# Attention scores of two heads in the two halves of TensorE's rows, and attention in rounds

## The chip, the cores and the metric

The kernel runs on one core of one Trainium2 chip. The metric is the device time of one execution in microseconds; the time of a kernel is the median of its runs. Engine names are those of the profile: PE is TensorE's matmul, PEld its weight load, DVE VectorE, ACT ScalarE, POOL GpSimd, SP the queue engine that issues most DMAs.

## What is computed

One layer of a hybrid decoder on x (1, 512, 1024), in float32:

```python
h = rms_norm(x, norm_w);  proj = h @ w_in                     # 1024 -> 4096, eight parts of 512
hq, hf, hi, hg, aq, ak, av, ag = split(proj)
o_h = rms_norm(hgrn2(hq, hf, hi)) * silu(hg)                  # 4 heads, gated linear recurrence
q, k = rms_norm(heads(aq)), rms_norm(heads(ak))               # 8 heads of width 64
s = q @ k.T * 64**-0.5 - slope * (t - s_pos);  causal         # 512 keys: own block of 256 and all past ones
o_a = softmax(s) @ heads(av) * silu(ag)
out = x + concat(o_h, o_a) @ w_out
```

With 512 positions and blocks of 256 a query's own block and its selected past blocks are all keys up to its position, so the attention is plain causal attention with a distance penalty (ALiBi).

## The kernel before

Tokens are cut in four tiles of 128, and everything large goes through TensorE. To keep float32 precision at the speed of the format fp32r, an operand is split into a high part (rounded to fp32r by ScalarE) and a low part (the rest, by VectorE), and a product is a sum of passes: high x high, high x low, low x high. Projections are eight groups of four units (`group`, `unit`); a unit accumulates 8 x 3 passes of 512 columns in one PSUM bank. The last groups are K (group 5), Q (6) and V (7); after them comes the output product in two parts, `out_h` for the recurrence's half of the mixed width and `out_a` for attention's half.

**The order on TensorE is written out** by a small planner inside the kernel: each pass adds its planned time to `clock[0]`, the projections and `out_h` are a filler that yields after every three passes (planned 0.648), and side work runs in generators (threads) that name the time and the `done` keys they wait for. Before each filler step, `drive` runs a thread that is ready by the planner's clock; when the filler is at its end, it advances the clock to the next thread. A `done` key holds the planner's time at which the instructions were issued. The other engines' queues are ordered by a scheduler at build time. At run time each engine works through its queue in order and waits at semaphores.

**K and Q.** `ev_qk` normalizes a unit's 128 tokens, and 14.29 later on the planner's clock `qk_tr` transposes them (four transpositions into one PSUM tile). Rows 0 to 63 of the result belong to the even head of each pair, rows 64 to 127 to the odd one. For each of the two heads of a pair (j) ScalarE and VectorE write high and low parts on 64 partitions, and a DMA on SP's queue copies them to the other 64: so the K tile of a head holds K high twice, KL holds K low twice, and the Q tile holds Q high over Q low. One pass over 128 rows then gives (Qhigh + Qlow) Khigh, and another (Qhigh + Qlow) Klow.

**Attention** goes by pairs of heads (p = 0 to 3) and units c = 3p + (0, 1, 2): query tile 3 (512 keys), tile 2 (384), tiles 1 and 0 (256 + 128). Each unit is one thread (`attn_unit`): scores of the two heads (`mm` into PSUM tiles `sc`, pool `psc` of four banks); minimum with the bias on VectorE (line 665), exponential with its sum on ScalarE (668), reciprocal on VectorE (671), product on GpSimd (673); then transpositions into two `tp` tiles of the pool `ptr` (two banks, line 55), copied by ScalarE to SBUF (682); then products with V, each head writing its half of the columns of `ot` (697). The units are spawned when the filler has gone through V (`start_attention`, line 951), a unit's scores wait by the planner for the transpositions of two units before, and products come for two units together. When all four tiles of a pair are done, VectorE multiplies `ot` by the gate (706) and the result is split for the output product (707, 708).

Lines that the change touches or that the prediction speaks of: 55, 148 (`LAT`), 568 to 589 (`qk_tr`), 597 to 621, 623 to 629, 635 to 715, 733 to 747 (`out_fin`: the residual's loads on GpSimd's and SP's queues, into the buffer that `hTl` leaves after V), 872, 949 to 953.

Of the kernel before, what the change touches and what calls it, by code (L numbers as in the profile page):

```python
# [1 line left out]

# [6 lines left out]
F32 = mybir.dt.float32  # L9
F32R = mybir.dt.float32r  # L10
I32 = mybir.dt.int32
AF = mybir.ActivationFunctionType
ALU = mybir.AluOpType
# [8 lines left out]
def kernel(  # L22
# [35 lines left out]
    def scratch(dt=F32):  # L58
        return scr.tile([P, 512], dt, tag="scr", name="scr")
# [85 lines left out]
            split_lo(n)  # L145

    POOL_LO = (3,)
    LAT = dict(lm=4.544, lev0=9.2567, lev=4.4882, copy=1.9908, rms=5.7036, silu=15.1764, qk=14.2881, soft=2.5598, softn=0.0041, acopy=4.5215, st=1.5748, ch=6.6909, DEPTH=2)
    SEQ = ('v0 y7 nt A0 s00 k00 y1 s10 k10 a0 H00 H10 B0 b0 H01 H11 t10 l10 L00 L10 L01 L11 wh1 t01 p20 q20 wl1 l01 '
           't11 p30 q30 l11 p01 q01 t02 p11 q11 l02 wh2 t12 l12 p21 q21 wl2 t03 l03 p31 q31 sq0 wh3 p02 q02 wl3 sq1 '  # L150
           't13 l13 p12 q12 sq2 p22 q22 sq3 rs p32 q32')
# [416 lines left out]
    def qk_tr(key, u, nrm, gain):  # L568
        yield LAT["qk"]
        tp = ptr.tile([P, 512], F32, tag="tr", name="tp")  # L570
        for j in range(NP):
            tr(tp[:, j * P:(j + 1) * P], nrm[:, j * P:(j + 1) * P])
        tpr = tp.rearrange("p (j t) -> p j t", t=P)
        ts_ = slice(u * P, (u + 1) * P)
        low = None if key == "K" else scratch(F32R).rearrange("p (j t) -> p j t", t=P)
        for j in range(2):
            lo = A["KL", j][:, :, ts_] if key == "K" else low
            own = slice(j * DH, (j + 1) * DH)
            oth = slice((1 - j) * DH, (2 - j) * DH)
            dst = A[key, j]  # L580
            nc.scalar.activation(dst[own, :, ts_], tpr[own], AF.Copy, scale=gain[own])
            nc.vector.scalar_tensor_tensor(lo[own], tpr[own], gain[own], dst[own, :, ts_].bitcast(F32),
                                           op0=ALU.mult, op1=ALU.subtract)
            if key == "K":
                for z in (dst, A["KL", j]):
                    nc.sync.dma_start(out=z[oth, :, ts_].bitcast(F32), in_=z[own, :, ts_].bitcast(F32))
            else:
                nc.sync.dma_start(out=dst[oth, :, ts_].bitcast(F32), in_=lo[own].bitcast(F32))
        done[(key, u)] = clock[0]

    A = {}
# [5 lines left out]
    def ev_qk(key, tags, gain):  # L597
        def ev(u, ps):
            if u == 0:
                wait_for("chunks")  # L600
                if key == "K":
                    for j in range(2):
                        A[key, j] = big.tile([P, NP, T], F32R, tag=tags[j], name=f"{key}{j}")
                        A["KL", j] = big.tile([P, NP, T], F32R, tag=tags[2 + j], name=f"KL{j}")
                else:
                    Q = big.tile([P, 2, NP, T], F32R, tag=tags[0], name=key)
                    for j in range(2):
                        A[key, j] = Q[:, j]
            sq = scratch()
            nc.scalar.activation(sq, ps, AF.Square, scale=rst[:, u:u + 1])  # L610
            ss = small.tile([P, 8], F32, tag="ss8", name="ss8")
            nc.vector.tensor_reduce(ss, sq.rearrange("p (h e) -> p h e", e=DH), axis=AX.X, op=ALU.add)
            r = rstd_of(ss, DH, 8)
            r2 = small.tile([P, 8], F32, tag="r2", name="r2")
            nc.gpsimd.tensor_tensor(r2, r, rst[:, u:u + 1].to_broadcast([P, 8]), op=ALU.mult)
            nrm = scratch()
            nc.vector.tensor_tensor(nrm.rearrange("p (h e) -> p h e", e=DH),
                                    ps.rearrange("p (h e) -> p h e", e=DH),
                                    r2.unsqueeze(2).to_broadcast([P, AH, DH]), op=ALU.mult)
            spawn(qk_tr(key, u, nrm, gain))  # L620
        return ev

    def ev_v(u, ps):
        if u == 0:
            wait_for(*[("read", n) for n in range(NT)])
            A["v"] = big.tile([P, NT, 512], F32, tag="G", name="vt")
        nc.scalar.activation(A["v"][:, u, :], ps, AF.Copy, scale=rst[:, u:u + 1])
        if u == 1:
            nc.scalar.activation(warm, A["v"][:, u, 0:1], AF.Exp, scale=0.0)


    UNITS = ((3,), (2,), (1, 0))
    DEPTH = LAT.get("DEPTH", 2)

    def attn_unit(c, p, tiles, ctx_):
        need = [("K", u) for u in range(tiles[0] + 1)] + [("Q", i) for i in tiles]
        if c >= DEPTH:
            need.append(("sdone", c - DEPTH))
        yield (0.0, *need)
        if "bias" not in ctx_:  # L640
            bias = big.tile([P, 2, T], F32, tag="at", bufs=2, name="bias")
            for j in range(2):
                nc.gpsimd.tensor_scalar(bias[:, j, :], A["Dm"], 2.0 ** (-8.0 * (2 * p + j + 1) / AH), 1.0,
                                        op0=ALU.mult, op1=ALU.mult)
            ctx_["bias"] = bias
        bias = ctx_["bias"]
        cols = []
        at = 0
        for i in tiles:
            cols.append((i, at, (i + 1) * P))  # L650
            at += (i + 1) * P
        m = len(tiles)
        zs = []
        for j in range(2):
            sc = psc.tile([P, 512], F32, tag="sc", name="sc")
            for i, o, n in cols:
                ts_ = slice(i * P, (i + 1) * P)
                us = max(0.109, n / 2370.0)
                mm(sc[:, o:o + n], A["Q", j][:, p, ts_], A["K", j][:, p, 0:n], True, False, us)
                mm(sc[:, o:o + n], A["Q", j][:, p, ts_], A["KL", j][:, p, 0:n], False, True, us)  # L660
            z = scratch()
            nm = small.tile([P, 2], F32, tag="nm", name="nm")
            l = small.tile([P, 2], F32, tag="l", name="l")
# [7 lines left out]
            nc.vector.reciprocal(rl[:, 0:m], l[:, 0:m])  # L671
            for e, (i, o, n) in enumerate(cols):
                nc.gpsimd.tensor_scalar(z[:, o:o + n], z[:, o:o + n], rl[:, e:e + 1], 1.0, op0=ALU.mult, op1=ALU.mult)  # L673
            zs.append(z)
        yield LAT["soft"] + at * LAT["softn"]
        pts = []
        for j in range(2):
            tp = ptr.tile([P, 512], F32, tag="tr", name="tp")
            for s in range(at // P):
                tr(tp[:, s * P:(s + 1) * P], zs[j][:, s * P:(s + 1) * P])  # L680
            pt = scratch()
            nc.scalar.copy(pt[:, 0:at], tp[:, 0:at])
            pts.append(pt)
        done[("sdone", c)] = clock[0]

        yield (LAT["acopy"], ("sdone", c | 1), *[(7, u) for u in range(tiles[0] + 1)])
        if "ot" not in ctx_:
            ctx_["ot"] = psc.tile([P, 512], F32, tag="sc", name="ot")
            ctx_["left"] = NT
        ot = ctx_["ot"]  # L690
        vt = A["v"]
        for i, o, n in cols:
            ts_ = slice(i * P, (i + 1) * P)
            for s in range(i + 1):
                for j in range(2):
                    hc = slice((2 * p + j) * DH, (2 * p + j + 1) * DH)
                    mm(ot[j * DH:(j + 1) * DH, ts_], vt[:, s, hc], pts[j][:, o + s * P:o + (s + 1) * P],
                       s == 0, s == i, 0.115)
        ctx_["left"] -= m
        if ctx_["left"] == 0:  # L700
            if "a" not in mT:
                mTa = big.tile([P, 2, NP, T], F32R, tag="hTh", name="mTa")
                mT["a"] = (mTa[:, 0], mTa[:, 1])
            mTah, mTal = mT["a"]
            mx = scratch()
            nc.vector.tensor_tensor(mx, ot, gT[:, p, :], op=ALU.mult)
            nc.scalar.copy(mTah[:, p, :], mx)
            nc.vector.tensor_sub(mTal[:, p, :], mx, mTah[:, p, :].bitcast(F32))
            done[("pair", p)] = clock[0]

    def start_attention():
        for p in range(NP):
            c_ = {}
            for m, tiles in enumerate(UNITS):
                spawn(attn_unit(p * len(UNITS) + m, p, tiles, c_))


    res = {}
# [146 lines left out]
    def fill_a():  # L865
        const_tri()
        yield from group(1, True, ev_f)
        yield from group(2, True, ev_silu_t(q2[:, 0]))
        yield from group(3, False, ev_silu(G))
        yield from group(4, True, ev_silu_t(gT))  # L870
        const_dist()
        yield from group(5, False, ev_qk("K", ("f", "k", "i", "KL"), kgs))
        yield from group(6, False, ev_qk("Q", ("q",), qgs))
        yield from group(7, False, ev_v)

    with tc.manual_schedule(engines={mybir.EngineType.PE}):
# [71 lines left out]

        def filler():
            yield from fa  # L950
            start_attention()
            wait_for(*[("read", n) for n in range(NT)])
            yield from out_h()

# [30 lines left out]
```

## Time and profile before

| | |
|---|---|
| runs | 290.51 us median of 3 (290.44 to 290.64) |
| profiled execution | 290.15 us, its span 288.3 us |
| granted TensorE clock | 1.00 |
| TensorE busy | 283.4 us, 98% of the span |
| VectorE, ScalarE, GpSimd busy | 173.3, 131.9, 63.4 us |
| passes and other matmul records | 1947 |

Matmul records overlap (a pass of 512 columns is listed with 0.39 us and follows the one before by 0.23), so a busy share of TensorE tells that it always had work, and the time a pass costs is read from the distance of starts or from the chain of waits, whose pieces do not overlap. Other records overlap a little as well.

### The profile page before, as it was taken

Reading aid. Unit: us, or ns where it says so; the run is one execution under the profiler, and the core shown is the slowest. Engines: PE = TensorE matmul, PEld = TensorE weight load, DVE = VectorE, ACT = ScalarE, POOL = GpSimd, SP = SyncE. Lnnn points to the kernel's source line nnn. Section 1 sums busy time; section 2 is a strip of 40 time slices with the busy share of each in tenths; the row PEclk is TensorE's granted clock in tenths of the full one; section 3 lists DMA queues with packets and bytes.
Section 4 is the critical chain, followed back from the end, with each engine's and each line's share of the span. In section 5 each row is a group of like instructions: output and inputs, shape, how many; then the busy total and the mean of one; then the engine's idle time right before and its main releaser. Section 6 shows DMA issues by size and latency. Waiting matters only on the chain.

```text
span 288.3 us, 5069 instructions
## 1 busy us (share of the span) xinstructions
PE 283.4 (98%) x1947; PEld 235.0 (82%) x1947; DVE 173.3 (60%) x374; ACT 131.9 (46%) x244; POOL 63.4 (22%) x102
## 2 busy tenths in 40 slices
PE   8999999999999999999999999999999999999995
PEld 6788788888887777898888888888888888888884
DVE  2952743734899998167855785485384677543232
ACT  5469623611601484125521743654675797652000
POOL 5006001191000000010273223420034655320000
PEclk9999999999999999999999999999999999999999
DMA  7990682430440008000610099558279000000132
GB/s 239 322 378 9 25 229 77 166 126 0 154 142 2 2 13 279 5 0 9 226 59 0 15 250 198 122 144 230 48 194 328 8 2 0 2 2 2 73 112 106
DMA packets 22152, 31.00 MB, mean 108 GB/s; under 512 B 1764, under 2 KB 9712, under 8 KB 22128
## 3 DMA queue, kind: packets, MB, share of 16 engines
q1 hardware_dynamic: 21056, 28.58, 34.7%
q0 software_dynamic: 512, 1.05, 1.2%
q10 hardware_dynamic: 560, 1.05, 1.0%
q8 instruction: 15, 0.25, 0.3%
q14 instruction: 9, 0.07, 0.1%
HBM read 25.17 MB, written 2.10 MB: 95 GB/s over the span
## 4 chain that ended last, share of the span: by engine, by line
PE 96%; DVE 1%; DMA 1%; issue 0%; ACT 0%; SPq 0%
PE acc L200 76%; PE tp L204 7%; PE sc L200 3%; PE ot L200 3%; PE pl L200 3%; PE ops L200 2%; DMA vec<-in_norm_w_dram 1%; PE us L200 1%; DVE wlo L124 0%; ACT hTh L304 0%; DVE hTl L293 0%; DVE res L781 0%; SPq L75 0%; DVE hTl L312 0%; DVE part L826 0%
## 5 line engine op out<-in xcount | busy, mean ns | idle before, releaser
L200 PE MATMUL acc<-whi,hTh 128*128 128x512 f32 x160 | 65.2, 407 | 0.0
L200 PE MATMUL acc<-whi,hTl 128*128 128x512 f32 x160 | 62.9, 393 | 0.3 <-DVE hTl L293 0.2
L200 PE MATMUL acc<-wlo,hTh 128*128 128x512 f32 x160 | 59.8, 391 | 0.0
L138 DVE TENSOR_TENSOR wlo<-raw,whi 128x1024 fp32r<-128x1024 f32 x38 | 46.1, 1236 | 7.1 <-ACT whi L130 6.6
L130 ACT CAST whi<-raw 128x1024 fp32r<-128x1024 f32 x39 | 40.5, 1048 | 13.6 <-DMA raw<-in_w_in_dram 6.2
L190 POOL TENSOR_TENSOR r<-v,mh 128x8 f32<-128x8 f32 (+1 forms) x12 | 17.2, 1430 | 99.2 <-DVE v L188 99.1
L200 PE MATMUL acc<-hTh,whi 128*128 128x512 f32 x96 | 38.2, 397 | 0.0
L200 PE MATMUL acc<-hTh,wlo 128*128 128x512 f32 x96 | 37.5, 391 | 0.0
L200 PE MATMUL acc<-hTl,whi 128*128 128x512 f32 x96 | 37.4, 389 | 0.0
L200 PEld LDWEIGHTS acc<-whi,hTl 128*128 128x128 f32 x160 | 30.1, 188 | 7.6 <-DVE hTl L312 0.9
L200 PEld LDWEIGHTS acc<-whi,hTh 128*128 128x128 f32 x160 | 30.1, 188 | 6.0
L200 PEld LDWEIGHTS acc<-wlo,hTh 128*128 128x128 f32 x160 | 30.0, 188 | 5.7
L673 POOL TENSOR_SCALAR scr<-scr,rl 128x512 f32<-128x512 f32 (+3 forms) x32 | 17.7, 562 | 18.4 <-DVE rl L671 14.8
L200 PEld LDWEIGHTS acc<-hTh,wlo 128*128 128x128 f32 x96 | 18.0, 188 | 4.0 <-DVE wlo L138 0.2
L200 PEld LDWEIGHTS acc<-hTh,whi 128*128 128x128 f32 x96 | 18.0, 188 | 3.6
L200 PEld LDWEIGHTS acc<-hTl,whi 128*128 128x128 f32 x96 | 18.0, 188 | 3.5
L745 DVE TENSOR_TENSOR res<-acc,res 128x512 f32<-128x512 f32 x15 | 10.3, 690 | 17.3 <-PE acc L200 14.6
L200 PE MATMUL acc<-whi,mTa 128*128 128x512 f32 (+1 forms) x72 | 20.4, 367 | 0.0
L668 ACT ACTIVATE scr<-scr,nm 128x512 f32<-128x512 f32 (+3 forms) x32 | 17.7, 555 | 3.4 <-DVE nm L665 2.0
L204 PE MATMUL tp<-ident,scr 128*128 128x128 f32 x128 | 18.2, 275 | 0.0
L204 PEld LDWEIGHTS tp<-ident,scr 128*128 128x128 f32 x128 | 14.9, 140 | 3.1 <-issue 0.7
L665 DVE CUSTOM_DVE_ANT_0 scr<-sc,bias 128x512 f32<-128x512 f32 (+3 forms) x32 | 14.1, 485 | 4.9 <-PE sc L200 4.9
(148 smaller groups left out, 430.8 us busy)
## 6 DMA issues: line engine op xcount, KB each, us to landing
raw<-in_w_in_dram SPq DMA_DIRECT2D x30, 512.0 KB, 4.7
raw<-in_w_out_dram SPq DMA_DIRECT2D x8, 512.0 KB, 6.0
out_dram<-res SPq DMA_DIRECT2D x7, 256.0 KB, 2.1
x<-in_x_dram SPq DMA_DIRECT2D x8, 128.0 KB, 4.3
x<-in_x_dram SPq DMA_DIRECT2D x4, 256.0 KB, 5.0
K<-K SPq DMA_DIRECT2D x8, 128.0 KB, 6.4
KL<-KL SPq DMA_DIRECT2D x8, 128.0 KB, 5.9
Q<-scr SPq DMA_DIRECT2D x8, 128.0 KB, 2.4
```

Source lines behind the costliest of these rows:

```text
L130: nc.scalar.copy(hi, raw)
L138: eng.tensor_sub(lo, raw, hi.bitcast(F32))
L190: nc.gpsimd.tensor_tensor(r, v, mh[:, 0:n], op=ALU.pow)
L200: nc.tensor.matmul(o, a, b, start=start, stop=stop)
L204: nc.tensor.transpose(o, a, ident)
L665: nc.vector.tensor_tensor_reduce(out=z[:, o:o + n], in0=sc[:, o:o + n], in1=bias[:, j, T - n:T], op0=ALU.add, op1=ALU.min, scale=1.0, scal ...
L668: nc.scalar.activation(z[:, o:o + n], z[:, o:o + n], AF.Exp, bias=nm[:, e:e + 1], scale=-1.0, accum_out=l[:, e:e + 1])
L673: nc.gpsimd.tensor_scalar(z[:, o:o + n], z[:, o:o + n], rl[:, e:e + 1], 1.0, op0=ALU.mult, op1=ALU.mult)
L745: nc.vector.tensor_tensor(res[hf][:, u, :], ps, res[hf][:, u, :], op=ALU.add)
```

## The change

- **Layout of K and Q.** `qk_tr` writes high and low parts for all 128 partitions at once: one ScalarE and one VectorE instruction for each tile of K or Q in place of two and two. The DMAs between partitions go. K, KL (buffers `f`, `k`) and Q, QL (halves of `q`) hold the two heads of a pair in the two halves of the partitions.
- **Scores.** A head's tile is three passes over its own 64 rows (Q K, Q KL, QL K), the two heads of a pair alternating, each in its own PSUM tile.
- **Rounds.** One thread, `attention`, spawned at the second unit of V (in `ev_v`), works in eight rounds of two units: products with V for the units of two rounds before, scores of this round's units, gate of the products, transpositions and copies of the round before's units, softmax of this round's. Round 0 waits by the planner for all units of K and Q with no added time, round 1 comes 5.0 after it, later ones 4.0 after the one before and after V's last unit.
- **ScalarE's order.** The exponentials of a round are bound behind its last copy of transposed tiles (`issue_after`).
- **Products** go to tiles of the pool `ptr` and are gated and split for each unit, in place in the gate's tile; the copies of transposed tiles go to buffers `i` and `KL`.

```diff
-        for j in range(2):
-            lo = A["KL", j][:, :, ts_] if key == "K" else low
...
-            nc.scalar.activation(dst[own, :, ts_], tpr[own], AF.Copy, scale=gain[own])
-            nc.vector.scalar_tensor_tensor(lo[own], tpr[own], gain[own], dst[own, :, ts_].bitcast(F32),
-                                           op0=ALU.mult, op1=ALU.subtract)
-            if key == "K":
-                for z in (dst, A["KL", j]):
-                    nc.sync.dma_start(out=z[oth, :, ts_].bitcast(F32), in_=z[own, :, ts_].bitcast(F32))
-            else:
-                nc.sync.dma_start(out=dst[oth, :, ts_].bitcast(F32), in_=lo[own].bitcast(F32))
+        hi, lo = A[key], A[key + "L"]
+        nc.scalar.activation(hi[:, :, ts_], tpr, AF.Copy, scale=gain)
+        nc.vector.scalar_tensor_tensor(lo[:, :, ts_], tpr, gain, hi[:, :, ts_].bitcast(F32),
+                                       op0=ALU.mult, op1=ALU.subtract)
...
         if u == 1:
             nc.scalar.activation(warm, A["v"][:, u, 0:1], AF.Exp, scale=0.0)
+            spawn(attention())
...
+    def scores(c):
...
+        scs = [psc.tile([P, 512], F32, tag="sc", name="sc") for _ in range(2)]
+        for i, o, n in cols:
+            ts_ = slice(i * P, (i + 1) * P)
+            for t, (a, b) in enumerate((("Q", "K"), ("Q", "KL"), ("QL", "K"))):
+                for j in range(2):
+                    own = slice(j * DH, (j + 1) * DH)
+                    mm(scs[j][:, o:o + n], A[a][own, p, ts_], A[b][own, p, 0:n], t == 0, t == 2,
+                       max(0.055, n / 4740.0))
...
+    def turn(c):
...
+            pts[m] = big.tile([P, 4, 512], F32, tag=("i", "KL")[m % 2], name="pt")
         for j in range(2):
             tp = ptr.tile([P, 512], F32, tag="tr", name="tp")
+            z = zs.pop((c, j))
             for s in range(at // P):
+                tr(tp[:, s * P:(s + 1) * P], z[:, s * P:(s + 1) * P])
+            last = nc.scalar.copy(pts[m][:, 2 * (c % 2) + j, 0:at], tp[:, 0:at])
+        return last
+
+    def attend(c):
+        p, cols, at = cols_of(c)
+        ot = ptr.tile([P, 512], F32, tag="tr", name="ot")
...
+    def gate(p, lo, w, ot):
...
+        mx = gT[:, p, lo:lo + w]
+        nc.vector.tensor_tensor(mx, ot[:, 0:w], mx, op=ALU.mult)
+        nc.scalar.copy(mTah[:, p, lo:lo + w], mx)
+        nc.vector.tensor_sub(mTal[:, p, lo:lo + w], mx, mTah[:, p, lo:lo + w].bitcast(F32))
+
+    def attention():
+
+        for m in range(NU // 2 + 2):
+            if m == 0:
+                yield (0.0, *[("K", u) for u in range(NT)], *[("Q", u) for u in range(NT)])
+            elif m == 1:
+                yield LAT["two"]
+            else:
+                yield (LAT["round"], *[(7, u) for u in range(NT)])
+            outs = [attend(c) for c in (2 * m - 4, 2 * m - 3) if m >= 2]
+            news = [(c, *scores(c)) for c in (2 * m, 2 * m + 1) if c < NU]
+            for z in outs:
+                gate(*z)
+
+            if 1 <= m <= NU // 2:
+                turn(2 * m - 2)
+                last = turn(2 * m - 1)
+            with tc.issue_after(last.ins) if m >= 1 else nullcontext():
+                for z in news:
+                    soft(*z)
...
-            start_attention()
```

`soft(c, ...)` holds lines 661 to 674 of before unchanged.

## Rows read from the trace of the kernel before

**Rows 1.** Page: busy us, share, instructions by engine; chain's shares by engine

```profile
PE 283.4 (98%) x1947; PEld 235.0 (82%) x1947; DVE 173.3 (60%) x374; ACT 131.9 (46%) x244; POOL 63.4 (22%) x102
...
PE 96%; DVE 1%; DMA 1%; issue 0%; ACT 0%; SPq 0%
```

**Rows 2.** Busy us (instructions) in a stretch, clock, DMA share, GB/s

```profile
211.50:262.90 51.40, 51.40 (x402) 43.81 (x400) 30.89 (x106) 34.25 (x95) 22.35 (x40) 1.00 0.23 72
```

**Rows 3.** Chain of waits, 211.5 to 262.9 us: shares by engine and line

```profile
by line: PE acc L200 44.3%; PE sc L200 19.5%; PE ot L200 18.8%; PE tp L204 18.6%
```

**Rows 4.** Pieces of that chain: start us, us, engine, tile, line, instructions

```profile
218.66 0.87 PE tp L204 x8
219.53 0.87 PE sc L200 x8
...
222.01 3.42 PE acc L200 x15
...
226.08 0.71 PE sc L200 x4
226.79 1.68 PE ot L200 x28
...
262.89 22.16 PE acc L200 x108
```

**Rows 5.** A piece of the chain earlier, on the whole array

```profile
117.85 0.89 PE us L200 x8
```

**Rows 6.** Timeline of PE: start us, us, line, op, tiles, array part, records

```profile
87.23 0.39 PE L200 MATMUL acc<-whi,hTl 128*128 128x512 f32 x1
87.55 1.10 PE L200 MATMUL pl<-q,k 128*32 128x64 f32 x64
88.58 0.50 PE L200 MATMUL acc<-whi,hTh 128*128 128x512 f32 x1
88.92 0.40 PE L200 MATMUL acc<-wlo,hTh 128*128 128x512 f32 x1
...
118.93 0.47 PE L200 MATMUL acc<-hTh,whi 128*128 128x512 f32 x1
119.24 0.39 PE L200 MATMUL acc<-hTl,whi 128*128 128x512 f32 x1
```

**Rows 7.** Timeline of all engines behind the last transpositions of Q

```profile
204.12 0.60 PE L204 MATMUL tp<-ident,scr 128*128 128x128 f32 x4
...
204.75 0.68 ACT L581 ACTIVATE Q<-tp,qgs 64x512 fp32r<-64x512 f32 x1 [1.61 <-PE tp L204]
...
205.47 0.74 DVE L582 SCALAR_TENSOR_TENSOR scr<-tp,qgs,Q 64x512 fp32r<-64x512 f32 x1 [3.05 <-ACT Q L581]
```

**Rows 8.** Tile tp, evacuations on 128 partitions: ns min/median/max, starts, forms

```profile
L562 ACT ACTIVATE mThh<-tp,col x4: 670/689/691, 129.9 to 159.4; 128x512 fp32r<-128x512 f32 x4
L563 DVE SCALAR_TENSOR_TENSOR mThl<-tp,col,mThh x4: 741/743/745, 130.6 to 162.5; 128x512 fp32r<-128x512 f32 x4
```

**Rows 9.** Timeline of PE and ACT at a unit's transpositions; line 682

```profile
218.50 1.03 PE L204 MATMUL tp<-ident,scr 128*128 128x128 f32 x8
...
219.13 1.07 ACT L682 COPY scr<-tp 128x512 f32<-128x512 f32 x2 [1.57 <-PE tp L204]
...
223.29 0.83 ACT L682 COPY scr<-tp 128x384 f32<-128x384 f32 x2
...
L682 ACT COPY scr<-tp x24: 457/482/593, 219.1 to 260.1; 128x384 f32<-128x384 f32 x16, 128x512 f32<-128x512 f32 x8
```

**Rows 10.** Groups by line: xcount | busy us, mean ns | idle before

```profile
L668 ACT ACTIVATE scr<-scr,nm 128x512 f32<-128x512 f32 (+3 forms) x32 | 17.7, 555 | 3.4 <-DVE nm L665 2.0 <-DMA res<-in_x_dram 1.3
...
L668 ACT ACTIVATION_READ_ACCUMULATOR scr<-scr,nm 128x1 f32 x32 | 6.0, 188 | 0.0
...
L673 POOL TENSOR_SCALAR scr<-scr,rl 128x512 f32<-128x512 f32 (+3 forms) x32 | 17.7, 562 | 18.4 <-DVE rl L671 14.8
```

**Rows 11.** DMA issues: tiles, queue, xcount, KB each, us to landing

```profile
res<-in_x_dram POOLq DMA_DIRECT2D x4, 256.0 KB, 8.3
```

More of the change, by code (lines that the diff above doesn't have):

```diff
@@ L1 @@
-from contextlib import ExitStack
+from contextlib import ExitStack, nullcontext
 import concourse.bass as bass
@@ L147 @@
     POOL_LO = (3,)
-    LAT = dict(lm=4.544, lev0=9.2567, lev=4.4882, copy=1.9908, rms=5.7036, silu=15.1764, qk=14.2881, soft=2.5598, softn=0.0041, acopy=4.5215, st=1.5748, ch=6.6909, DEPTH=2)
+    LAT = dict(lm=4.544, lev0=9.2567, lev=4.4882, copy=1.9908, rms=5.7036, silu=15.1764, qk=14.2881, two=5.0, round=4.0, st=1.5748, ch=6.6909)
     SEQ = ('v0 y7 nt A0 s00 k00 y1 s10 k10 a0 H00 H10 B0 b0 H01 H11 t10 l10 L00 L10 L01 L11 wh1 t01 p20 q20 wl1 l01 '
@@ L574, in qk_tr @@
         ts_ = slice(u * P, (u + 1) * P)
-        low = None if key == "K" else scratch(F32R).rearrange("p (j t) -> p j t", t=P)
-        for j in range(2):
-            lo = A["KL", j][:, :, ts_] if key == "K" else low
-            own = slice(j * DH, (j + 1) * DH)
-            oth = slice((1 - j) * DH, (2 - j) * DH)
-            dst = A[key, j]
-            nc.scalar.activation(dst[own, :, ts_], tpr[own], AF.Copy, scale=gain[own])
-            nc.vector.scalar_tensor_tensor(lo[own], tpr[own], gain[own], dst[own, :, ts_].bitcast(F32),
-                                           op0=ALU.mult, op1=ALU.subtract)
-            if key == "K":
-                for z in (dst, A["KL", j]):
-                    nc.sync.dma_start(out=z[oth, :, ts_].bitcast(F32), in_=z[own, :, ts_].bitcast(F32))
-            else:
-                nc.sync.dma_start(out=dst[oth, :, ts_].bitcast(F32), in_=lo[own].bitcast(F32))
+        hi, lo = A[key], A[key + "L"]
+        nc.scalar.activation(hi[:, :, ts_], tpr, AF.Copy, scale=gain)
+        nc.vector.scalar_tensor_tensor(lo[:, :, ts_], tpr, gain, hi[:, :, ts_].bitcast(F32),
+                                       op0=ALU.mult, op1=ALU.subtract)
         done[(key, u)] = clock[0]
@@ L601, in ev @@
                 if key == "K":
-                    for j in range(2):
-                        A[key, j] = big.tile([P, NP, T], F32R, tag=tags[j], name=f"{key}{j}")
-                        A["KL", j] = big.tile([P, NP, T], F32R, tag=tags[2 + j], name=f"KL{j}")
+                    A[key], A[key + "L"] = (big.tile([P, NP, T], F32R, tag=t, name=n)
+                                            for t, n in zip(tags, (key, key + "L")))
                 else:
                     Q = big.tile([P, 2, NP, T], F32R, tag=tags[0], name=key)
-                    for j in range(2):
-                        A[key, j] = Q[:, j]
+                    A[key], A[key + "L"] = Q[:, 0], Q[:, 1]
             sq = scratch()
@@ L629, in ev_v, with cols_of @@
             nc.scalar.activation(warm, A["v"][:, u, 0:1], AF.Exp, scale=0.0)
+            spawn(attention())
     UNITS = ((3,), (2,), (1, 0))
[L633 to L646, printed above, removed]
+    NU = NP * len(UNITS)
+    def cols_of(c):
+        p, tiles = c // len(UNITS), UNITS[c % len(UNITS)]
         cols = []
@@ L651, in attn_unit, with soft @@
             at += (i + 1) * P
-        m = len(tiles)
-        zs = []
-        for j in range(2):
[L655 to L660, printed above, removed]
+        return p, cols, at
+    zs = {}
+    pts = {}
+    def scores(c):
+        p, cols, at = cols_of(c)
+        if c % len(UNITS) == 0:
+            bias = big.tile([P, 2, T], F32, tag="at", bufs=2, name="bias")
+            for j in range(2):
+                nc.gpsimd.tensor_scalar(bias[:, j, :], A["Dm"], 2.0 ** (-8.0 * (2 * p + j + 1) / AH), 1.0,
+                                        op0=ALU.mult, op1=ALU.mult)
+            A["bias"] = bias
+        bias = A["bias"]
+        scs = [psc.tile([P, 512], F32, tag="sc", name="sc") for _ in range(2)]
+        for i, o, n in cols:
+            ts_ = slice(i * P, (i + 1) * P)
+            for t, (a, b) in enumerate((("Q", "K"), ("Q", "KL"), ("QL", "K"))):
+                for j in range(2):
+                    own = slice(j * DH, (j + 1) * DH)
+                    mm(scs[j][:, o:o + n], A[a][own, p, ts_], A[b][own, p, 0:n], t == 0, t == 2,
+                       max(0.055, n / 4740.0))
+        return p, cols, at, scs, bias
+    def soft(c, p, cols, at, scs, bias):
+        m = len(cols)
+        for j in range(2):
+            sc = scs[j]
             z = scratch()
@@ L673, in attn_unit @@
                 nc.gpsimd.tensor_scalar(z[:, o:o + n], z[:, o:o + n], rl[:, e:e + 1], 1.0, op0=ALU.mult, op1=ALU.mult)
-            zs.append(z)
-        yield LAT["soft"] + at * LAT["softn"]
-        pts = []
+            zs[c, j] = z
+    def turn(c):
+        p, cols, at = cols_of(c)
+        m = c // 2
+        if c % 2 == 0:
+            pts[m] = big.tile([P, 4, 512], F32, tag=("i", "KL")[m % 2], name="pt")
         for j in range(2):
             tp = ptr.tile([P, 512], F32, tag="tr", name="tp")
+            z = zs.pop((c, j))
             for s in range(at // P):
[L680 to L690, printed above, removed]
+                tr(tp[:, s * P:(s + 1) * P], z[:, s * P:(s + 1) * P])
+            last = nc.scalar.copy(pts[m][:, 2 * (c % 2) + j, 0:at], tp[:, 0:at])
+        return last
+    def attend(c):
+        p, cols, at = cols_of(c)
+        ot = ptr.tile([P, 512], F32, tag="tr", name="ot")
         vt = A["v"]
+        lo = min(i for i, _, _ in cols) * P
+        w = len(cols) * P
         for i, o, n in cols:
-            ts_ = slice(i * P, (i + 1) * P)
             for s in range(i + 1):
@@ L696, in attn_unit @@
                     hc = slice((2 * p + j) * DH, (2 * p + j + 1) * DH)
[L697 to L715, printed above, removed]
+                    mm(ot[j * DH:(j + 1) * DH, i * P - lo:i * P - lo + P], vt[:, s, hc],
+                       pts[c // 2][:, 2 * (c % 2) + j, o + s * P:o + (s + 1) * P], s == 0, s == i, 0.115)
+        return p, lo, w, ot
+    def gate(p, lo, w, ot):
+        if "a" not in mT:
+            mTa = big.tile([P, 2, NP, T], F32R, tag="hTh", name="mTa")
+            mT["a"] = (mTa[:, 0], mTa[:, 1])
+        mTah, mTal = mT["a"]
+        mx = gT[:, p, lo:lo + w]
[20 more added lines that the diff above has]
+                    soft(*z)
     res = {}
@@ L871, in fill_a @@
         const_dist()
-        yield from group(5, False, ev_qk("K", ("f", "k", "i", "KL"), kgs))
+        yield from group(5, False, ev_qk("K", ("f", "k"), kgs))
         yield from group(6, False, ev_qk("Q", ("q",), qgs))
```

## Prediction

> **What bounds the kernel now.** First the busy shares and the chain that ended last: the page gives TensorE 98% of the span, and the chain runs 96% through it [rows 1]. Then the busy time by stretch: from 211.5 to 262.9 us, the stage that the change rewrites, TensorE is busy for 51.40 of 51.40 us, VectorE for 30.9, ScalarE for 34.3, GpSimd for 22.4 [rows 2]. So the time is the sum of TensorE's pitches: time goes only where its work shrinks, and every wait put in front of it is paid in full, since no slack exists to swallow it.
>
> In the chain the stage is one unbroken row of TensorE pieces: 44.3% projections, 19.5% scores, 18.8% products with V, 18.6% transpositions [rows 3]. Scores: 10.0 us. The pieces give the price of one pass (one instruction over all rows): 0.228 us at 512 columns (15 in 3.42), 0.178 at 384 (4 in 0.71), 0.109 as mean of 256 and 128 (8 in 0.87) [rows 4]. A pair of heads costs 4(0.228 + 0.178) + 8 x 0.109 = 2.50; four pairs make the 10.0.
>
> **Scores.** A head and query tile now takes three passes over 64 rows in place of two over 128; the two heads use different row halves and different PSUM tiles. If the halves run at once, a pair of heads costs 3(0.228 + 0.178) + 6 x 0.109 = 1.87, four pairs 7.5: a gain of 2.5. If nothing overlaps it is twice that, 14.9: a loss of 4.9. No instruction of the kernel before works on row halves side by side. The nearest row is the products with V, on column halves: 28 records in 1.68 us, 0.060 each, against 0.111 for the same 128-column records on the whole array (8 in 0.89) [rows 4, 5]. That is 1.85-fold, and 14.9 / 1.85 = 8.1: I take a gain of 1.9.
>
> **Changes of array shape.** A run on a part of the array costs 0.09 us going in (87.23 to 87.55 us is 0.32 where a pass takes 0.23) and 0.11 coming out (88.58 to 88.92) [rows 6]. Before, six blocks of products with V make 12 such changes. After, the score blocks change shape too: two changes in rounds 0 and 1, three in rounds 2 to 5, two each in rounds 6 and 7, 20 in all: 8 x 0.1 = 0.8 more. Against it, the first pass after a group of transpositions comes 0.08 late (118.93 to 119.24, where 0.23 is usual) [rows 6], and 12 groups become six: 0.5 back. Net +0.3; from -0.3 (score shape free) to +1.2 (0.3 or so in and out of the score shape, half as much again as here).
>
> **Round 0 starts right behind the last transposition of Q.** Before, the first scores came after the whole V projection. Now the attention thread is spawned at V's second tile, asks only for K and Q, with no added time, and the planner marks Q done when its transpositions are *issued*. So the first score passes stand directly behind them on TensorE, and pair 0's tile 3 needs just these columns. In the trace ScalarE takes the transposed tile at 204.75 for 0.68, VectorE writes the low part from 205.47 to 206.21 [rows 7]. With 128 partitions these two cost the same as with 64 there: 0.689 and 0.743 for the like pair at lines 562 and 563 [rows 8]. TensorE has issued the last of four transpositions by 204.56; the high part lets it start at 205.5 (0.94 idle), two terms fill 0.46, the third waits for the low part until 206.27 (0.31): 1.25 us. From 0.9 (only the first wait) to 2.0 (a 0.7 us evacuation stands ahead on ScalarE).
>
> **Two transposition buffers for four tiles.** A round now transposes two units x two heads, four tiles back to back, on a pool of two PSUM buffers: the third tile waits until ScalarE has copied the first. Before, a unit's two tiles were followed by other TensorE work. From the rows: eight transpositions issue from 218.50, pitch 0.109 (0.87 for eight), and the copy of the first four starts at 219.13, 0.63 later; two copies take 1.07 at 512 columns, 0.83 at 384, each alone 0.593 and 0.482 [rows 4, 9]. Tiles of 4, 4, 3, 3 blocks: the first copy ends at 0.63 + 0.59 = 1.22, and with 0.05 for the signal the third tile starts at 1.27 and not 0.87: 0.40; the second copy ends at 1.76, the fourth tile starts at 1.81 and not 1.60: 0.21; together 0.61. By the same steps 3, 3, 4, 4 loses 0.40 and 3, 3, 3, 3 loses 0.50. Each order comes twice in six rounds: 3.0 us. From 1.5 (half of each hidden, weights being loaded meanwhile) to 5 (another 0.35 a round, where a cast of a gated tile stands ahead of the copies). The products' two tiles take the same two buffers, and VectorE must have gated them before the first transposition: the scores, 1.2 us, lie between, so nothing.
>
> **What is costed at nothing.** (1) Q and K lose 8 ScalarE and 8 VectorE instructions of 0.68 and 0.75 us and 24 copies between partitions on the SP queue: TensorE waits for none of them; weight loads behind them only come earlier. (2) The exponentials wait for the round's last copy. Behind them on ScalarE, casts of gated tiles and weights; behind those, VectorE's reciprocals and GpSimd's products, which the next round's transpositions need. Counted from a round's last score: shape change and transpositions 2.1, last copy done at 2.8, exponentials 3.9 at most (32 of 0.555 and 32 sum reads of 0.188 over six rounds), then a reciprocal (some 0.2) and two GpSimd products of 0.562 [rows 10]: 8.0 at most. The cover: planner steps are 0.648, so it puts 8, 9, 7, 7, 7, 4 and 0 steps of projections between the rounds (10 steps of V and 32 of the first output half are left after round 0). Seven steps are 4.8 us, with 2.1 of transpositions, 1.7 of products and 1.2 of scores 9.8: enough. Before round 6 only four steps are left: 2.1 + 2.7 + 1.7 = 6.5, and its last tile is wanted some 1.4 later, 7.9: even. Without the cover the wait would be the difference, up to 1 us. (3) The last round's gate, some 2 us, lies under 18 passes of the output, 4.1. (4) The residual's loads wait on GpSimd's and SP's queues for the end of V, now some 6 us later; they land 8.3 us after issue [rows 11], and the third output tile, which needs the first one's buffer back, comes 10.5 us after the end of V (7 steps, round 2, one step).
>
> **Sum.** -1.9 + 0.3 + 1.25 + 3.0 = +2.65 on the profiled execution's 290.15 (span 288.3, 1.85 around it): 292.8. The median of the runs is 0.36 above it: 293.2.
>
> **Rivals.**
> A. *Faster: the row halves overlap whole and the two-buffer waits mostly vanish.* The deciding place is the third tile of a round's transpositions. If TensorE loses 0.2 per round there and not 0.5, the sum is -2.5 (scores) - 0.3 + 0.9 + 1.2 = -0.7: 289.8. It tips when a round's loss falls under some 0.3. For it: TensorE shows no wait on a copy in 288 us, and six transposition groups fewer. Against it: the order on TensorE is written out, with nothing between second and third tile.
> B. *The weight loads of the halves follow one another.* In the 256/128 pieces the 1,536 columns would take 0.68 at the 512-column rate and took 0.87 [rows 4]: a pass costs at least about 0.109. With six loads a query tile, 6 x 0.109 = 0.65 is the floor (12 for the two short tiles together): 0.68 + 0.65 + 1.31 = 2.65 a pair, 10.6: scores lose 0.6. Sum +5.15: 295.7. Against it: 64 records on 32-column parts took 1.03 us [rows 6], far below that floor each.
> The Trainium skill (TensorE: Matmul & The Clock Gate, Part 3, "Measured speedup vs the span model") gives four row tiles 3.07-fold rather than 4-fold. By that share two halves would give 1.53-fold, an estimate of 9.8 us for the scores and 294.9 for the kernel, near this rival; no run here shows row tiles yet.
> C. *The halves don't overlap, the change doesn't do what it says.* Scores 14.9: sum +9.45, 300.0. Against it: column halves do overlap.
>
> **How the numbers follow.** Forecast 0.56, with its own range 291.5 to 295.7 (terms' ends combined, not all at once); A 0.20; B 0.12; C 0.07; 0.05 for others. What a measurement here can tell from no change is about 0.2%, 0.6 us. A gives nearly all of faster, 0.20; same 0.10 comes from the low end of the forecast and the upper of A; slower 0.70 from the rest. Range 289.4 to 297.5: C and the lower part of A stay out.
>
> **What would show it.** Score passes of two heads starting almost together, a 512-column pair every 0.23 to 0.26 us: the gain (right), every 0.45: C. TensorE idle about 1.2 us behind Q's last transpositions at about 204.6, ended by ScalarE and then VectorE. In rounds 1 to 6 TensorE idle 0.4 to 0.6 us within the transpositions, ended by the copies at the line of the round's copy. The output's last part should start some 2.6 us later than 262.89 [rows 4]. If TensorE shows no wait at those two places, the forecast is wrong.

## The result, and the profile after

The changed kernel takes 300.98 us in the median (300.64 to 301.01), the kernel before 290.51 in the same comparison: a ratio of 1.0344, 95% interval 1.0323 to 1.0366. Slower was forecast, but 293.2 in a range up to 297.5: the direction was right, the size was not.

The page of the kernel after, its busy shares (TensorE, VectorE, ScalarE) and the chain's shares by engine; they answer to [rows 1]:

```profile
span 299.2 us, 5068 instructions
...
PE 287.3 (96%) x1979; PEld 234.6 (78%) x1979; DVE 168.9 (56%) x382; ACT 127.7 (43%) x244; POOL 63.1 (21%) x102
...
PE 90%; DMA 3%; ACT 2%; DVE 2%; issue 1%; POOLq 0%; POOL 0%; SPq 0%; ACTq 0%; DVEq 0%
```

TensorE's share fell from 98% to 96%. The chain, which before ran through nothing but TensorE in the stage, now has 3% of DMA, 2% of ScalarE and 2% of VectorE over the whole span (before: 1%, 0% and 1%). The waits of TensorE in the stage, none before (us in total, times, longest):

```profile
PE acc L200 <- DVE res L762: 3.7, 1, 3.7
PE tp L204 <- ACT pt L686: 2.0, 6, 0.3
...
PE sc L200 <- ACT Q L576: 0.8, 1, 0.8
PE tp L204 <- POOL scr L672: 0.5, 1, 0.5
```

The second, third and fourth were forecast in kind. The first, the longest, was not. The chain of waits after, around it and at the start of the output's last part (start us, us, what):

```profile
218.73 5.29 DMA res<-in_x_dram
...
224.12 0.70 DVE res L762
...
224.87 4.21 PE acc L200 x9
229.07 2.41 PE ot L200 x28
...
273.75 0.43 PE acc L200
```

The output's last part starts at 273.75, before at 262.89 [rows 4]: 10.86 later, and the span is 10.9 longer. So the loss lies whole in the rewritten stage. TensorE's timeline in that place (start us, us, line, tiles, array part, records, [idle before <- what ended it]):

```profile
218.27 0.39 PE L200 MATMUL acc<-whi,mThh 128*128 128x512 f32 x1
...
220.77 0.39 PE L200 MATMUL acc<-whi,mThl 128*128 128x512 f32 x1
224.87 0.80 PE L200 MATMUL acc<-whi,mThh 128*128 128x512 f32 x1 [3.71 <-DVE res L762]
225.46 0.63 PE L200 MATMUL acc<-wlo,mThh 128*128 128x512 f32 x1
225.88 0.63 PE L200 MATMUL acc<-whi,mThl 128*128 128x512 f32 x1
```

From 218.27 the first output tile gets its 12 passes. The first pass of the *second* tile stands until 224.87: it waits for the addition of the residual (VectorE, line 762) that empties the first tile's PSUM bank, and that addition waits for a load (218.73, 5.29 us). Passes then follow each other by 0.427 us, where 0.228 is usual. The window of these passes (columns as in [rows 2]):

```profile
224.80:229.00 4.20, 4.13 (x9) 2.81 (x9) 1.14 (x2) 0.00 (x0) 0.00 (x0) 0.50 0.37 142
```

The granted clock is 0.50, the level of 1.2 GHz; it fell during the 3.7 us without work.

Where the time went is added up from the starts of TensorE's groups in the timeline, from Q's last transpositions (204.12 before, 204.23 after) to the first pass of the output's last part; a group's time is the distance to the next group's start, its waits included. `e1` is the first experiment below.

| us, start to start | before | after | e1 |
|---|---|---|---|
| Q's last transpositions | 0.35 | 1.37 | 1.38 |
| scores | 10.93 | 9.07 | 9.07 |
| transpositions | 8.10 | 12.92 | 12.92 |
| products with V | 9.64 | 10.36 | 9.63 |
| projections | 29.67 | 35.73 | 29.84 |
| sum | 58.69 | 69.45 | 62.84 |

In e1, which differs from after in two lines of the table and has no wait for the residual, the stage is 4.15 longer than before; the forecast was 2.65. The 6.6 on top are the wait and what the clock lost behind it: the pass at 224.87 is 3.87 late (221.00 was its turn, 0.23 after 220.77), the nine passes take some 2.0 more, the products with V behind them 0.73.

The forecast's other signs, in the same timeline: round 0, round 1's transpositions, and a score block of a later round:

```profile
204.23 0.60 PE L204 MATMUL tp<-ident,scr 128*128 128x128 f32 x4
205.60 0.50 PE L200 MATMUL sc<-K,Q 64*128 64x512 f32 x2 [0.78 <-ACT Q L576]
205.94 0.40 PE L200 MATMUL sc<-KL,Q 64*128 64x512 f32 x2
206.39 0.68 PE L200 MATMUL sc<-K,Q 64*128 64x512 f32 x4
...
214.61 1.09 PE L204 MATMUL tp<-ident,scr 128*128 128x128 f32 x8
216.03 1.00 PE L204 MATMUL tp<-ident,scr 128*128 128x128 f32 x6 [0.33 <-ACT pt L686]
...
241.46 0.50 PE L200 MATMUL sc<-K,Q 64*128 64x512 f32 x2
241.79 0.40 PE L200 MATMUL sc<-KL,Q 64*128 64x512 f32 x2
242.02 0.57 PE L200 MATMUL sc<-K,Q 64*128 64x512 f32 x4
```

"x2" are the passes of two heads with one start; the next pair comes 0.23 later (241.79, 242.02), the pitch of one pass before. The halves overlap whole. The third tile of round 1's transpositions starts 1.42 after the first, where eight at pitch take 0.87.

### The profile page after: what moved, and what is told of

Same layout as the page of the kernel before. It is cut to its first block, busy times and chain, and to the rows that moved or that the text cites. A ratio compares the mean times of both kernels' runs of the same rounds, so it can differ in the third digit from the quotient of the medians.

```text
span 299.2 us, 5068 instructions
## 1 busy us (share of the span) xinstructions
PE 287.3 (96%) x1979; PEld 234.6 (78%) x1979; DVE 168.9 (56%) x382; ACT 127.7 (43%) x244; POOL 63.1 (21%) x102
## 4 chain that ended last, share of the span: by engine, by line
PE 90%; DMA 3%; ACT 2%; DVE 2%; issue 1%; POOLq 0%; POOL 0%; SPq 0%; ACTq 0%; DVEq 0%
PE acc L200 72%; PE tp L204 6%; PE ot L200 3%; PE sc L200 3%; PE pl L200 3%; PE ops L200 2%; DMA res<-in_x_dram 2%; ACT pt L686 1%; DMA vec<-in_norm_w_dram 1%; PE us L200 1%; ACT scr L667 1%; DVE res L762 0%; DVE wlo L124 0%; DVE hTl L312 0%; DVE Q L577 0%
## 5 line engine op out<-in xcount | busy, mean ns | idle before, releaser
L672 POOL TENSOR_SCALAR scr<-scr,rl 128x512 f32<-128x512 f32 (+3 forms) x32 | 16.8, 536 | 37.8 <-DVE rl L670 37.6
L204 PE MATMUL tp<-ident,scr 128*128 128x128 f32 x128 | 18.9, 277 | 2.4 <-ACT pt L686 2.0
L200 PE MATMUL acc<-whi,mThh 128*128 128x512 f32 x32 | 13.7, 429 | 3.7 <-DVE res L762 3.7
```

Source lines behind the costliest of these rows:

```text
L200: nc.tensor.matmul(o, a, b, start=start, stop=stop)
L204: nc.tensor.transpose(o, a, ident)
```

## The experiments

e0 and e1 start from the kernel after, e3 from the kernel before, e2, e4 and e5 from e1; e6, e7 and e8 build on these. Each ratio stands against runs of the kernel before on the same chip.

**e1_v_on_vector: V's last tile leaves PSUM through VectorE.** In the kernel after, ScalarE empties V's last accumulator only behind round 1's exponentials and a weight's cast. From ScalarE's timeline after:

```profile
220.63 1.04 ACT L130 CAST whi<-raw 128x1024 fp32r<-128x1024 f32 x1
221.56 0.69 ACT L615 ACTIVATE vt<-acc,rst 128x512 f32<-128x512 f32 x1
```

```diff
-        nc.scalar.activation(A["v"][:, u, :], ps, AF.Copy, scale=rst[:, u:u + 1])
+        if u == 3:
+            nc.vector.tensor_scalar(A["v"][:, u, :], ps, rst[:, u:u + 1], 1.0, op0=ALU.mult, op1=ALU.mult)
+        else:
+            nc.scalar.activation(A["v"][:, u, :], ps, AF.Copy, scale=rst[:, u:u + 1])
```

> The changed kernel with the evacuation of V's last unit on VectorE, everything else and the bond as changed. Theory S: VectorE is idle there, V's bank is free at once, the second output tile takes it, no wait for the residual's add and no half clock: 300.98 - 6.3 = 294.7. Rival L: the second tile, or the third, waits for the residual just the same: 300 to 301.

Measured: 295.12 us (294.37 to 295.29), ratio 1.0139 [1.0108, 1.0170]. TensorE's timeline where the second output tile begins, then VectorE's with V's last tile, then the first tile's addition in the chain of waits:

```profile
221.00 0.39 PE L200 MATMUL acc<-whi,mThh 128*128 128x512 f32 x1
```

```profile
218.64 0.73 DVE L616 TENSOR_SCALAR vt<-acc,rst 128x512 f32<-128x512 f32 x1
```

```profile
223.59 0.06 DVE res L765
```

The wait for the residual is gone. The second tile starts at 221.00, ahead of the first one's addition at 223.59, so it has the other bank, the one that V left at 219.37. The granted clock is 1.00 over the run, and the other waits are as they were (1.9, 0.8 and 0.5). That is 5.9 us between the medians (300.98 and 295.12), the cost of the low clock included: without the wait it does not come.

**e0_no_bond: the exponentials are not bound behind the copies**, all else as after.

```diff
-            with tc.issue_after(last.ins) if m >= 1 else nullcontext():
+            with nullcontext():
```

> The changed kernel without the bond that puts a round's exponentials behind its copies; all else as changed. Theory S (slot): the 3.7 us wait and the half clock behind it come because V's last evacuation stands behind round 1's bound exponentials on ScalarE, so that the second output tile gets the first one's PSUM bank. Without the bond the wait of 3.7 us and the 2.6 us at half clock go: 300.98 - 6.3 = 294.7, up to 298 if exponentials now stand ahead of copies and lengthen the waits in the transpositions (0.7 us in each of five rounds). Rival L (load): the residual's loads are too late in any case, because V ends 6 us later: still about 301.

Measured: 308.73 us (306.38 to 309.81), ratio 1.0607 [1.0538, 1.0676]: 10.7 above the upper end of what was expected. TensorE's waits in the stage, ScalarE's order in round 1, and TensorE's third tile there:

```profile
PE tp L204 <- ACT pt L686: 6.6, 4, 2.2
PE tp L204 <- POOL bias L642: 2.3, 1, 2.3
PE tp L204 <- POOL scr L672: 1.9, 1, 1.9
```

```profile
216.18 0.51 ACT L667 ACTIVATE scr<-scr,nm 128x256 f32<-128x256 f32 x1 [1.70 <-DVE nm L664]
...
217.57 1.05 ACT L686 COPY pt<-tp 128x512 f32<-128x512 f32 x2
```

```profile
214.90 1.09 PE L204 MATMUL tp<-ident,scr 128*128 128x128 f32 x8
218.28 1.51 PE L204 MATMUL tp<-ident,scr 128*128 128x128 f32 x6 [2.28 <-POOL bias L642]
...
220.02 0.63 PE L200 MATMUL acc<-wlo,hTh 128*128 128x512 f32 x1
220.44 0.63 PE L200 MATMUL acc<-whi,hTl 128*128 128x512 f32 x1
```

The residual's wait went here too: the second output tile starts at 224.52, ahead of the first one's addition at 226.88. V's last tile leaves PSUM later than in the kernel after (222.96 to 223.64 for 221.56 to 222.25), but TensorE is later still. In the traces of before, e0 and e1 V had left its bank before the second tile's turn (212.30 for 215.78, 223.64 for 224.52, 219.37 for 221.00), and the tile got that bank; in the kernel after V had not (222.25 for 221.00), and the tile got the first one's. That agrees with theory S; how the program's allocation chooses a bank was not tried by itself. In exchange the exponentials, themselves late behind VectorE, stand ahead of the copies, and TensorE's third tile waits for the copy that starts at 217.57 and, at 0.59 for the first, ends at 218.16. (The wait is listed under GpSimd's bias, which ended about then, but no transposition reads it.) The three lines are some 11 us of waits, and after 2.28 us of idleness passes are again 0.42 apart. The binding in the change is worth more than the 7.8 us between the two kernels, since this one lacks the residual's wait.

**e2_heads_in_turn: e1, and one head's three passes come before the other's.**

```diff
-            for t, (a, b) in enumerate((("Q", "K"), ("Q", "KL"), ("QL", "K"))):
-                for j in range(2):
+            for j in range(2):
+                for t, (a, b) in enumerate((("Q", "K"), ("Q", "KL"), ("QL", "K"))):
```

> As e1, but each head's three score passes one after the other, then the other head's, and not alternating. If the halves overlap only where neighbours on TensorE's queue use different halves, the 48 query-tile passes no longer overlap, scores cost 14.9 in place of 7.5: e1 plus 6 to 7.5, 301 to 302. If TensorE starts passes of the other half past waiting ones: as e1, 294.7.

Measured: 295.47 us, ratio 1.0160 [1.0127, 1.0193], as e1. The theory that heads must alternate for their halves to overlap falls. Only round 0's scores are longer (2.21 for 1.75, start to start), the later blocks as in e1 (1.59, 1.36, 1.42). Its round 0 in TensorE's timeline:

```profile
205.55 0.50 PE L200 MATMUL sc<-K,Q 64*128 64x512 f32 x1 [0.78 <-ACT Q L576]
...
206.34 0.50 PE L200 MATMUL sc<-K,Q 64*128 64x512 f32 x2
206.68 0.38 PE L200 MATMUL sc<-KL,Q 64*128 64x512 f32 x1
206.68 0.33 PE L200 MATMUL sc<-K,Q 64*128 64x384 f32 x1
...
206.90 0.57 PE L200 MATMUL sc<-K,Q 64*128 64x512 f32 x3
```

At 206.68 the first head's 384-column tile starts beside the second head's second pass over 512 columns; in the program it stands behind the second head's third pass, which comes at 206.90. A wait, though, holds both halves. The "x2" at 206.34 are the first head's third pass, which waits for the low part from VectorE, and the second head's first pass, which needs only the high part that the first head used at 205.55. With the heads alternating it started beside the first head's (205.60 in the kernel after); the 0.46 of round 0 is this.

**e3_halves_alone: the kernel before with the new layout and the row-half scores, its units and order kept.** It leaves out rounds, binding and the gate by unit; the core of its edit in `attn_unit`:

```diff
-            for i, o, n in cols:
...
-                mm(sc[:, o:o + n], A["Q", j][:, p, ts_], A["K", j][:, p, 0:n], True, False, us)
-                mm(sc[:, o:o + n], A["Q", j][:, p, ts_], A["KL", j][:, p, 0:n], False, True, us)
+        for i, o, n in cols:
...
+            for t, (a, b) in enumerate((("Q", "K"), ("Q", "KL"), ("QL", "K"))):
+                for j in range(2):
+                    own = slice(j * DH, (j + 1) * DH)
+                    mm(scs[j][:, o:o + n], A[a][own, p, ts_], A[b][own, p, 0:n], t == 0, t == 2, ...)
```

> The kernel before with only the layout of K and Q and the scores in row halves; units, filler order, buffers as before, no rounds, no bond. Theory: row halves bring 2.5 and cost up to 12 blocks x 0.2 in shape changes, so between 288 and 290.5, and what was lost lies in the rounds. Rival: the halves themselves cost more than they bring: 291 or more.

Measured: 292.07 us, ratio 1.0052 [1.0029, 1.0075]: slower by half a per cent, outside the theory's 288 to 290.5 and within the rival's 291 or more, with no wait of TensorE in the stage. Its chain of waits at the place of [rows 4]:

```profile
220.23 0.87 PE tp L204 x8
221.10 0.84 PE sc L200 x9
221.94 0.81 PE tp L204 x6
222.74 0.89 PE sc L200 x5
```

Start to start, the stage is 59.99, 1.30 over before: scores -1.33, transpositions +1.86, projections +0.78. A score block of three pairs at 512 columns takes 0.89 where its passes are 3 x 0.228 = 0.68; six transpositions between two score blocks take 0.80, before 0.60. With 12 score blocks the changes of shape cost more than the overlap brings: 2.5 gained on the passes, 1.17 lost in the score blocks and 2.64 around them. Here the grouping in rounds shows its worth: six blocks, not 12.

**e4_late_round0: e1, and round 0 waits 2.0 more by the planner**, so that projections stand behind Q's last transpositions.

```diff
-                yield (0.0, *[("K", u) for u in range(NT)], *[("Q", u) for u in range(NT)])
+                yield (2.0, *[("K", u) for u in range(NT)], *[("Q", u) for u in range(NT)])
```

> e1 (V's last evacuation on VectorE) with 2.0 planned time between Q's last transpositions and round 0, four filler steps. If the wait behind Q's last transpositions is what the trace names it (ScalarE, then VectorE), it goes whole: e1's stage less 1.35 us, 293.8 or ratio 1.011. Rival: the filler put between only moves the wait to another place (V's end, the residual's loads): as e1, 295.1.

Measured: 293.72 us (293.33 to 293.92), ratio 1.0098 [1.0082, 1.0115]. Q's transpositions are back at 0.35 and the first scores at 1.42: the 1.02 on the one and 0.32 on the other, 1.34 together, are gone, and the median is 1.4 lower than e1's. (The trace's stage, 61.81, is 1.0 shorter: the projections, in one more piece, take 0.24 of it back.)

**e5_split_turns: e1, and a filler step of three passes between a round's two units of transpositions.**

```diff
                 turn(2 * m - 2)
+                yield 0.3
                 last = turn(2 * m - 1)
```

> e1 with one filler step (0.68 us of projections) between a round's two units of transpositions. Theory: rounds 1 to 5 lose 0.5 to 0.66 each over the pitch because four tiles share two PSUM buffers; with the step between them TensorE shows no wait on the copies there, and five rounds give back 0.35 to 0.45 each, less 0.08 for the change to projections: e1 less 1.4 to 1.9, 293.2 to 293.7; round 6 has no filler and stays. Rival: the loss is the change of the array's shape between scores and transpositions, which the step does not touch: as e1 or 0.4 slower.

Measured: 294.76 us (294.36 to 297.37), ratio 1.0141 [1.0118, 1.0165], as e1: 1.1 above the expected, and by its total the rival fits as well. The trace is of an execution of 297.37 us, 2.6 above the median, with a granted clock of 0.50 from 266.7 to 270.0, in rounds 6 and 7. Its waits in the stage:

```profile
PE tp L204 <- DVE gT L712: 1.3, 2, 1.0
PE tp L204 <- ACT pt L689: 1.1, 1, 1.1
...
PE tp L204 <- POOL scr L675: 0.5, 1, 0.5
```

The waits on copies are gone from rounds 1 to 5 (eight transpositions 0.85, three passes 0.78, six transpositions 0.57), so the mechanism holds and the rival falls; other waits took their place. The transpositions now also wait for VectorE's gate, since products use the same two buffers, and in this execution round 6, with less filler left, waits 1.1 for a copy.

**e6_all: e4 and e5 together, and rounds closer by the planner** (`round=2.55` for 4.0), so that the split costs no distance at the end.

> e1 with the late round 0, the split transpositions and a planned 2.55 between rounds in place of 4.0, so that the filler reaches round 6. If the terms add, e1 less 1.35, less 1.7, less 0.8 for round 6: 291.2, still 0.6 over the kernel before, which is the price of the array's changes of shape that row halves bring. If shorter rounds expose the exponentials (8 us from scores to the next transpositions): 292 to 294. Faster than before only if the shape changes cost less in this order than in e3: 290 or less.

Measured: 291.10 us, ratio 1.0013 [0.9996, 1.0030]: as before the change. What is left is 0.8 for the gate in round 4 and 0.5 for GpSimd's products in round 6. VectorE's timeline tells why the gate is late:

```profile
239.94 0.29 DVE L712 TENSOR_TENSOR gT<-ot,gT 128x128 f32<-128x128 f32 x1
240.50 2.36 DVE L138 TENSOR_TENSOR wlo<-raw,whi 128x1024 fp32r<-128x1024 f32 x2 [0.27 <-ACT whi L130]
...
242.98 0.42 DVE L712 TENSOR_TENSOR gT<-ot,gT 128x256 f32<-128x256 f32 x1
```

Two low parts of weights, 1.2 us each, stand between the gates of one round's two product tiles.

**e7_fill_round6: e6, and the time before round 6 is filled** (`{6: 4.0, 7: 0.3}` for these rounds' added time). **e8_fill_pool: e7, and GpSimd writes the low parts of weight tiles 38 and 39** (`POOL_LO = (3, 38, 39)`).

> e6 with three of the four filler steps between rounds 6 and 7 moved to between rounds 5 and 6. In e6 round 6's transpositions waited 0.45 us for GpSimd's products and lost 0.65; three steps more are 2 us, so this goes: e6 less 0.65, 290.5, the same as before. Rival: round 7 then waits for the copies of round 6 (no filler between): as e6, 291.1.

> e7 with the low parts of the last two weight blocks (2 x 1.2 us on VectorE) on GpSimd. In e6 round 4's transpositions waited 0.82 us for a gate that stood behind these on VectorE, 1.1 lost in all: less 1.1 again, 289.4, 1.1 under the kernel before. Rival: on GpSimd they take 2.4 us each and stand ahead of round 4's products: as e7 or slower.

Measured: e7 291.09 us, ratio 1.0008 [0.9990, 1.0027], so a miss by 0.6: round 6 lost the wait for GpSimd and got one for the gate. e8 290.28 us (289.96 to 291.64), ratio 0.9975 [0.9958, 0.9993]: 0.9 above its forecast, but the one version that beats both kernels, by a quarter of a per cent against the kernel before (290.86 in this comparison), an interval that barely leaves 1 out. Its only wait in the stage, and the stage in one window:

```profile
PE tp L204 <- DVE gT L712: 0.4, 1, 0.4
```

```profile
204.42:262.90 58.48, 58.03 (x468) 47.17 (x466) 37.41 (x123) 39.33 (x107) 26.40 (x42) 1.00 0.20 64
```

58.5 us against 58.69. Start to start, the scores gain 2.2; the transpositions take 0.8 of it back (0.4 for the gate) and the projections, cut in more pieces, 1.15.

## Why the prediction was wrong

**The step that failed is (4) of what was costed at nothing.** It took the *third* output tile as the one that needs the first one's buffer back, 10.5 us after V's end, and set the load's 8.3 us against that. It was the second, which was due 2.73 us after V's end (218.27 to 221.00). The load took 5.3, less than assumed, and the addition could start only at 224.12. That the pool's two buffers alternate holds in the trace before, where the second tile starts ahead of the first one's addition (timelines of TensorE and VectorE):

```profile
215.78 0.39 PE L200 MATMUL acc<-whi,mThh 128*128 128x512 f32 x1
...
218.62 0.69 DVE L745 TENSOR_TENSOR res<-acc,res 128x512 f32<-128x512 f32 x1 [1.66 <-DMA res<-in_x_dram]
```

That the change would leave it so was assumed. What the step lacks is V's last tile, which holds the other buffer: (2) lists what stands behind the bound exponentials on ScalarE and leaves this evacuation out, and it ends at 222.25, 1.25 after the second tile's turn. So even an alternating pool would have cost some 1.2 us, an estimate from these two times. The step names the right load and the right buffer and gives the buffer to the wrong tile. By the step's own numbers the right tile would have given a wait of 8.3 - 2.73 = 5.6 us for the load alone, and a forecast of 298.8. The lowered clock behind the wait, 2.7 us, was in no term. e1, without the wait and the low clock, measures 295.12, inside the forecast's own range of 291.5 to 295.7.

**Scores, -1.9: mis-sized, -2.5.** Six score blocks take 9.07, without round 0's wait 8.75; four pairs at whole overlap are 4 x 1.87 = 7.48, down from 10.0. The 1.85-fold from column halves was too careful. By the share that the Trainium skill (TensorE: Matmul & The Clock Gate, Part 3, "Measured speedup vs the span model") gives for four row tiles it would be 1.53-fold, an estimate; the pair's pitch of 0.23 us, that of one pass, contradicts this for two halves.

**Changes of shape, +0.3: right.** The six blocks take 8.75 - 7.48 = 1.27 over their passes, before it was 10.93 - 10.0 = 0.93 over: +0.34. Another 0.17 is on the projections and was in no term. The Trainium skill (TensorEngine Tiling (Array Packing), Key Properties) says that changing the tiling mode drains the engine; the 0.2 us per block agree, and e3 shows what 12 such blocks make.

**Round 0's wait, +1.25: right.** 1.02 on the transpositions and 0.32 between the score passes (0.22 from 205.94 to 206.39, where 0.23 is usual, and 0.1 on the pair behind it), together 1.34; e4 takes it away whole.

**Two buffers for four tiles, +3.0: place and mechanism right, size 4.8.** By round, transpositions are longer than before by 0.80, 0.60, 0.65, 0.76, 0.61 and 1.40. Rounds 1 to 5 lose 3.42 for a predicted 2.52; over the pitch of 0.109, by which the 2.52 was worked out, they lose 2.9 (10.30 for 68 transpositions). In round 1 the copy starts 0.69 after the first transposition (214.61 to 215.30) where 0.63 was taken, and the third tile 0.14 behind the copy's end where 0.05 was. (The sum puts the second copy's end at 1.76 where its own rows, 0.63 and 1.07, give 1.70; 1.77 was measured.) Round 6 loses 1.40 for 0.50; 0.45 of it is the wait for GpSimd's products that (2) called "even" and costed at nothing. e5 and e6 show that a filler step between the units takes this wait away, and what comes in its place.

**The rivals.** A fell at its own deciding place: a round loses 0.6 to 0.8 there. B fell: the block of 256 and 128 columns takes 0.84 in e3, where B has 1.31. C gave 300.0, a mere 1 us from the result, and is wrong: the halves overlap whole. A total that fits a rival does not show it; the pitch of the score pairs decides between them.

## What to carry to other kernels

When a step on the path is hidden by "its buffer is not needed yet", find out which tile gets which buffer in the built program, and when the one before leaves it, and price that; a pool of two need not alternate. In a stage where one engine is busy throughout, a change that saves 2 us on it must be priced at each place where it now meets a result only just issued: back-to-back tiles on two buffers, scores behind their own transpositions. Put a few independent passes between them, and then look which engine is late next.

## What the runs showed of the hardware

- **The two row halves work like two queues, until one waits for another engine.** In e2 a pass of one half started at 206.68, ahead of an earlier one of the other half at 206.90, and the order of the heads made no difference to the later blocks. The Trainium skill (TensorE: Matmul & The Clock Gate, Part 3, "The mechanism") has matmuls start in program order; on row halves this trace shows otherwise. So of TensorE it does not hold strictly that each engine works through its queue in order. A pass that waited for VectorE (206.34) held the other half's next pass with it.
- **One wait cost 1.7 times itself.** After 3.7 us without work the granted clock was 0.50 for the next nine passes, 2.7 us more; after 2.28 us in e0 passes were 0.42 apart too. The 0.78 us wait in round 0 was followed by the usual pitch, but in e5's trace the clock was 0.50 from 266.7 to 270.0, behind waits of no more than 0.5 and 1.1 us.
- **Changing the array shape cost about 0.2 us per score block**, and as much again on transpositions between two such blocks (0.80 for 0.60).
